# Experts of a two-block decoder layer: neighbouring rows per partition, g2 applied on GpSimd, scattered products added from PSUM

## The chip, the cores and the metric

The kernel runs on one core of a Trainium2 chip. The metric is the device time of one execution in microseconds. The engines are named as in the profile: PE (TensorE, with PEld for its weight loads), DVE (VectorE), ACT (ScalarE), POOL (GpSimd) and SP (SyncE, which issues the loads).

## The reference

Two blocks run one after the other over 256 tokens of 2048 values. The change lies in the last part, a mixture of 16 experts, of which each token uses two:

```python
def moe_ffn(h, router_w, router_bias, w_gate, w_up, w_down):
    ...
    combine = jnp.sum((esel[..., None] == jnp.arange(N_EXPERTS)) * w[..., None], axis=1)
    y = jnp.zeros_like(t)
    for e in range(N_EXPERTS):
        he = jax.nn.silu(t @ w_gate[e]) * (t @ w_up[e])
        y = y + combine[:, e:e + 1] * (he @ w_down[e])
    return y.reshape(b, s, d)
...
h = rmsnorm_2(x, norm2_g[l]) * (1.0 + sc2[:, None]) + sh2[:, None]
x = x + g2[:, None] * moe_ffn(h, router_w, ...)
return rmsnorm_2(x, final_g)
```

`w_gate` and `w_up` are 2048 x 512 for each expert, `w_down` is 512 x 2048, all in 32-bit floats: 4 MB each. `g2` is one row of 2048 values.

## The kernel before

Weights arrive as loads of 1 MB (128 partitions x 2048 values), issued by SP in order into a ring of buffers (`_load`, L128). A load is worked on in two chunks of 1024 columns. For five chunks of six `_split` makes a rounded copy on ACT (L146) and the rest, weight minus copy, on DVE (L147), and PE multiplies with both (L1914, L1915); every sixth chunk goes to PE whole (L1912). `run` hands out the order: it splits up to AHEAD = 4 chunks ahead, does one chunk's products, and then calls `step`, which takes one entry from each background queue. The order on every engine is the order in which the program emits its instructions; nothing is reordered later.

Between the mixers and the experts, `evac_out` adds the mixers' result to x (L1461), squares it (L1466) and multiplies x with its gain row on POOL to give h2 (L1467), in blocks of 512 columns for the two token tiles tt. `after_mix` then scales h2 and adds the row sh2, the first 1024 columns on DVE (L1784), the others on ACT and POOL (L1800, L1801), and picks the experts with some thirty small DVE instructions (L1795 to L1833) that PE waits for (L1836).

The experts go by pairs. `gather` multiplies h2, by blocks of 128 columns, with a selection matrix, so that the tokens of two experts stand as columns (L1898, L1904, L1905); it runs beside the first eight chunks of `down` of every even expert. In the order of emission stand gate and up of expert e (16 chunks) and then `down` of expert e - 1 (8 chunks). `give` adds the two halves of a down result (ACT L2055, DVE L2056) into the tile `out`, 64 rows for each expert of the pair. After `down` of every odd expert a pipeline of eight `scatter` items starts on the queue "out", for two token tiles and four blocks of 512 columns: PE multiplies the combine weights with `out` into a PSUM bank (L2119), DVE multiplies the bank with g2 (L2125), POOL adds that to x (L2129). An item moves on by one stage at each turn; a turn is every second chunk (pad = 1) for all pairs but the last scattered one, where it is every chunk. The pair of experts 14 and 15 is added by other code (`last`), which stays.

PSUM has eight banks; `bank` hands out the one that was given back first. Seven pairs are scattered in this way: 56 items.

Of the kernel before, what the change touches and what calls it, by code (L numbers as in the profile page):

```python
# [13 lines left out]
OP = mybir.AluOpType  # L14
# [3 lines left out]
D = 2048  # L18
# [27 lines left out]
class Kernel:  # L46
# [50 lines left out]
    def add(self, g):  # L97
        a = 0
        while a < len(g.kts):

            kk = min(g.kk if self.loads[1:] else 1, len(g.kts) - a)
            k0 = g.kts[a]
            src = g.w[k0 * 128:(k0 + kk) * 128, g.c0:g.c1].rearrange("(j p) c -> p j c", p=128)
            self.add_load(src, kk * g.C)
            for j in range(kk):
                self.add_chunk(j * g.C, g.C, lambda wh, wl, j=a + j: self._mm(g, j, wh, wl))
            self.count += 1
            if self.every and self.count % self.every == 0 and self.side:
                src, n, use = self.side.popleft()
                self.add_load(src, n)  # L110
                self.chunks.append([len(self.loads) - 1, 0, n, None, use, None])
            a += kk
# [1177 lines left out]
    def mixers(self):  # L1290
        nc, i = self.nc, self.i
        w = i["w_in_2"][0]
# [158 lines left out]
        def evac_out(c0, w):  # L1451
            def evac(b, ps):
                tt, n = divmod(b * 512, w)
                if c0 + b == 0:
                    self.h2 = [self.U(), self.U()]
                s = slice(c0 + n, c0 + n + 512)
                o, m = self.x[tt][:, s], M[c0 // 1024]
                n = s.start % 1024
                t = self.small([128, 512], "ev")
                nc.vector.tensor_mul(t, ps, m[:, n:n + 512])  # L1460
                (nc.vector if tt or c0 else nc.gpsimd).tensor_add(o, o, t)  # L1461
                k = tt * 4 + s.start // 512

                def rest():
                    j = self.small([128, 512], "pts", 4)
                    nc.scalar.activation(j, o, AF.Square, accum_out=self.s2[:, k:k + 1])  # L1466
                    nc.gpsimd.tensor_mul(self.h2[tt][:, s], o, m[:, 1024 + n:1536 + n])  # L1467
                if c0 == 1536:
                    rest()
                else:  # L1470
                    self.bg("out", rest)
                if tt == 1 and s.stop == c0 + w:
                    for kt in range(c0 // 128, s.stop // 128, 2):
                        self.bg("out", lambda kt=kt: self.logits(kt))
                    if c0 == 0:
                        self.bg("out", lambda: (self.free(M[0]), sh2()))
            return evac

        def sh2():
            self.sh2 = self.row(self.mod[3:4, :])  # L1480
# [290 lines left out]
    def after_mix(self):  # L1771

        nc, i = self.nc, self.i
# [5 lines left out]
        nc.vector.tensor_reduce(ss, self.s2[:, 0:8].rearrange("p (t k) -> p t k", t=2), axis=AX.X, op=OP.add)  # L1779
        r = self.rstd(ss, D, 2)  # L1780
        self.table(AF.Sigmoid)
        for tt in range(2):
            h = self.h2[tt][:, 0:1024]
            nc.vector.scalar_tensor_tensor(h, h, r[:, tt:tt + 1], self.sh2[:, 0:1024], op0=OP.mult, op1=OP.add)  # L1784
        t = self.small([128, 256], "ln")
        nc.scalar.copy(t[0:16, :], self.lg[0:16, 0:256])
        self.done(self.lg)
# [5 lines left out]
        for tt in range(2):  # L1793
            e = slice(tt * 16, tt * 16 + 16)
# [3 lines left out]
        for tt in range(2):  # L1798
            h = self.h2[tt][:, 1024:D]
            nc.scalar.activation(h, h, AF.Copy, scale=r[:, tt:tt + 1])  # L1800
            nc.gpsimd.tensor_add(h, h, self.sh2[:, 1024:D])  # L1801
        self.free(self.sh2)
        v3 = lambda t, n: t.rearrange("p (t e) -> p t e", e=n)
        bc = lambda t, n: t.unsqueeze(2).to_broadcast([128, t.shape[1], n])
# [9 lines left out]
        eq, m = sm(32, "req"), sm(2, "rm")  # L1814
# [102 lines left out]
    def experts(self):  # L1917
        nc, i = self.nc, self.i
        E = {}

        def after(q, n, f):
            for _ in range(n):
                self.bg(q, lambda: None)
            self.bg(q, f)

        def gate_up(e):
            st = E[e] = {}

            def mm(key, j, wh, wl):
                if j == 0:  # L1930
                    st[key] = self.bank()
                    if key == "g" and e % 2 == 0:
                        wt = weights(e)
                        after("gu", 3, lambda: turned(e, wt))
                for n in range(2):
                    x = self.XG[:, e % 2, j + n, :]
                    self.both(st[key], x, wh, wl, slice(n * 512, n * 512 + 512), j + n == 0, j + n == 15)
                if j == 0 and key == "g" and e % 2 == 1 and e < 15:
                    self.S = self.slots(e // 2 + 1)
                if j == 14:  # L1940
                    after("gu", 0, lambda: take(e, key))
                    after("gu", 4 if e < 15 else 0, lambda: fold(e, key))
                    if key == "u":
                        after("gu", 0, lambda: hidden(e))
                        after("gu", 1 if e < 15 else 0, lambda: parts(e))

            for key, w in (("g", "exp_w_gate_2"), ("u", "exp_w_up_2")):
                src = i[w][0, e].rearrange("(j p) n -> p j n", p=128)
                for j in range(0, 16, 4):
                    self.add_load(src[:, j:j + 4, :], 2048)  # L1950
                    for n in range(2):
                        self.add_chunk(n * 1024, 1024, lambda wh, wl, key=key, j=j + 2 * n: mm(key, j, wh, wl), n == 1 and whole())

        def whole():

            return len(self.loads) % 3 == 0
# [25 lines left out]
        def weights(e):  # L1982

            w = self.small([128, 256], "bias", 3)
            for tt in range(2):
                for n in range(2):
                    k = tt * 16 + e + n
                    nc.gpsimd.tensor_scalar(w[:, tt * 128 + n * 64:tt * 128 + n * 64 + 64], self.iota,
                                            self.pos_[:, k:k + 1], self.comb[:, k:k + 1],
                                            op0=OP.is_equal, op1=OP.mult)  # L1990
            return w
# [32 lines left out]
        def down(e):  # L2024
            src = i["exp_w_down_2"][0, e].rearrange("(j p) n -> p j n", p=128)
# [33 lines left out]
            def rows(j, c, wh, wl):  # L2059
                if j == 0 and c == 0:  # L2060
                    begin()
                for n in range(2):
                    mm(j, c * 2 + n, wh, wl, slice(n * 512, n * 512 + 512))
                if j == 3 and c == 1 and e % 2 == 1:
                    after("out", 3, lambda: None)
                    self.pipeline("out", [scatter(e - 1, tt, b) for tt in range(2) for b in range(4)], 1, e < 13)

            def columns(b, c, wh, wl):
                if b == 0 and c == 0:
# [36 lines left out]
            for n in range(4):  # L2106
                self.add_load(src[:, n:n + 1, :] if e < 15 else src[:, :, n * 512:n * 512 + 512], 2048)
                for c in range(2):
                    self.add_chunk(c * 1024, 1024,
                                   lambda wh, wl, n=n, c=c: (rows if e < 15 else columns)(n, c, wh, wl), c == 1 and whole())  # L2110

        def scatter(e, tt, b):
            s = slice(b * 512, b * 512 + 512)
            x = self.x[tt][:, s]
            st = {}

            def mm():
                ps = st["ps"] = self.bank()
                nc.tensor.matmul(ps, E[e]["ct"][:, tt * 128:tt * 128 + 128], E[e]["out"][:, s], start=True, stop=True)  # L2119
                if tt == 1 and b == 3:  # L2120
                    self.free(E[e]["out"])

            def mul():
                st["t"] = self.small([128, 512], "ev")
                nc.vector.tensor_mul(st["t"], st["ps"], self.g2[:, s])  # L2125
                self.done(st["ps"])

            def add():
                nc.gpsimd.tensor_add(x, x, st["t"])  # L2129
            return [mm, mul, add]  # L2130

        def new_block():
            self.XG = self.big.tile([128, 2, 16, 128], F32R, name=self.name("xg"), tag="big")
# [25 lines left out]
        for e in range(16):  # L2159
            n = len(self.chunks)  # L2160
# [5 lines left out]
            if e:  # L2166
                n = len(self.chunks)
# [5 lines left out]
    def overflow(self):  # L2173

        nc, i = self.nc, self.i
        for q in ("out", "end0", "end1", "end2", "end3"):
            self.flush(q)
        n = nc.values_load(self.most[0:1, 0:1], min_val=0, max_val=T)
        self.resize(-len(self.ring))
        hT, hid, wts = [self.U(), self.U()], self.U(), deque(self.U() for _ in range(3))  # L2180
        with self.tc.If(n > 64):
# [5 lines left out]
            for kt in range(NKT):  # L2187
                ps = self.bank()
# [10 lines left out]
                return wt  # L2199

            with self.tc.For_i(0, 16, 1) as e:
                w = {k: i[f"exp_w_{k}_2"][0][bass.ds(e, 1)].rearrange("a (j p) n -> p (a j) n", p=128)
                     for k in ("gate", "up", "down")}
                eq = self.small([128, 32], "req", 1)
                c = self.small([128, 2], "rm", 1)
                for tt in range(2):
# [16 lines left out]
                for b in range(2):  # L2223
                    t = self.small([128, 512], "ev")
                    o = hid[:, b * 512:b * 512 + 512]
# [4 lines left out]
                for tt in range(2):  # L2230
# [6 lines left out]
                    for b in range(4):  # L2237
                        t = self.small([128, 512], "ev")
                        s = slice(b * 512, b * 512 + 512)
                        nc.vector.tensor_mul(t, y[b], self.g2[:, s])  # L2240
                        x = self.x[tt][:, s]
                        nc.vector.scalar_tensor_tensor(x, t, c[:, tt:tt + 1], x, op0=OP.mult, op1=OP.add)
                        self.done(y[b])
            for tt in range(2):
                for b in range(4):
                    t = self.small([128, 512], "ev")
# [104 lines left out]
```

## Time and profile before

| what | value |
|---|---|
| median of three runs | 2854.59 us (2854.22 to 2856.4) |
| the profiled execution | 2856.04 us, of which the span 2854.3 us |
| PE, DVE, ACT, POOL busy in the span | 97%, 74%, 50%, 11% |
| granted TensorE clock, mean | 0.987 of 2.4 GHz |
| HBM read | 680.66 MB, 239 GB/s over the span |
| the experts, about | 2240 us to the end |
| loads of gate, up and down | 64 each, 1 MB each |

A row of groups gives line, engine, operation, what is written from what, the count, the busy time and the mean duration of one; then the idle time of the engine before them and who ended it. A row of waits gives who waited for whom, the total in us, the number of waits and the longest. A row of a window gives from and to, the length, the busy time and the count of instructions of each engine, the granted clock, the share of the 16 DMA engines and their rate.

### The profile page before, as it was taken

The page shows a single profiled execution, that of the slowest core. Times are in us where ns is not written, and L with a number is a line of the kernel's source. Part 1 is how long each engine was busy: PE and PEld are TensorE (multiplying, and loading weights), DVE is VectorE, ACT ScalarE, POOL GpSimd, SP SyncE. Part 2 cuts the span into 40 slices and gives each one's busy share as a digit, 9 for nine tenths or more (in the row PEclk, how much of TensorE's full clock was granted, in tenths as well). Part 3 has the DMA queues.
Part 4 walks back from the last instruction along what each step waited for, and adds up shares of the span by engine and source line. Part 5 has one row for each costly group of instructions (what it writes and reads, how often), then busy time and mean ns, then how long its engine had stood idle before and what let it go on. Part 6 is the DMA issues. An engine that isn't in the chain of part 4 may idle for free. (4 is left out here: it accounts for less than half of the span.)

```text
span 2854.3 us, 43859 instructions
## 1 busy us (share of the span) xinstructions
PE 2756.7 (97%) x17766; PEld 2410.4 (84%) x17766; DVE 2106.4 (74%) x2679; ACT 1418.5 (50%) x2100; POOL 315.8 (11%) x286
## 2 busy tenths in 40 slices
PE   8999999999999999999999998999999799999997
PEld 8898999999998999897989797988886676666664
DVE  5566558899767768877777786656555689998998
ACT  5433444334444545434444445345554476666665
POOL 0000100000100000001000102111001202222223
PEclk9999999999999999999999999999999899999999
DMA  7576555566667765676667573745555599989895
GB/s 256 193 275 247 199 215 166 176 235 214 248 233 266 259 228 221 239 263 216 257 216 267 195 253 128 265 128 195 179 202 173 209 372 337 342 324 343 322 342 211
DMA packets 201427, 685.77 MB, mean 240 GB/s; under 512 B 12148, under 2 KB 15332, under 8 KB 180356
## 3 DMA queue, kind: packets, MB, share of 16 engines
q1 hardware_dynamic: 194336, 662.94, 64.3%
q0 software_dynamic: 5680, 19.53, 2.5%
q8 instruction: 141, 2.31, 0.3%
q10 hardware_dynamic: 1203, 0.45, 0.1%
q14 instruction: 67, 0.54, 0.1%
HBM read 680.66 MB, written 2.20 MB: 239 GB/s over the span
## 5 line engine op out<-in xcount | busy, mean ns | idle before, releaser
L147 DVE TENSOR_TENSOR u<-u,u 128x1024 fp32r<-128x1024 f32 (+3 forms) x1064 | 1258.1, 1216 | 393.9 <-ACT u L146 392.2
L146 ACT CAST u<-u 128x1024 fp32r<-128x1024 f32 (+3 forms) x1064 | 1015.3, 995 | 615.6 <-DMA u<-in_w_in_dram 157.3
L181 PE MATMUL ps<-u,u 128*128 128x256 f32 (+1 forms) x2184 | 626.3, 287 | 2.6 <-ACT u L146 1.7
L183 PE MATMUL ps<-u,u 128*128 128x256 f32 (+1 forms) x2184 | 621.1, 284 | 2.5 <-DVE u L147 2.5
L182 PE MATMUL ps<-u,u 128*128 128x256 f32 (+1 forms) x2184 | 621.0, 284 | 0.5
L181 PE MATMUL ps<-big,u 128*128 128x256 f32 (+1 forms) x1672 | 481.4, 288 | 1.2 <-ACT big L1285 0.7
L183 PE MATMUL ps<-big,u 128*128 128x256 f32 (+1 forms) x1672 | 476.6, 285 | 4.3 <-DVE u L147 4.3
L182 PE MATMUL ps<-big,u 128*128 128x256 f32 (+1 forms) x1672 | 476.5, 285 | 0.1
L181 PEld LDWEIGHTS ps<-u,u 128*128 128x128 f32 (+1 forms) x2184 | 420.9, 193 | 11.9 <-issue 6.4
L183 PEld LDWEIGHTS ps<-u,u 128*128 128x128 f32 (+1 forms) x2184 | 420.7, 193 | 4.4 <-DVE u L147 4.3
L182 PEld LDWEIGHTS ps<-u,u 128*128 128x128 f32 (+1 forms) x2184 | 420.9, 193 | 1.7 <-DVE u L1286 1.3
L181 PEld LDWEIGHTS ps<-big,u 128*128 128x128 f32 (+1 forms) x1672 | 322.9, 193 | 13.5 <-issue 7.0
L183 PEld LDWEIGHTS ps<-big,u 128*128 128x128 f32 (+1 forms) x1672 | 322.9, 193 | 5.8 <-DVE u L147 5.6
L182 PEld LDWEIGHTS ps<-big,u 128*128 128x128 f32 (+1 forms) x1672 | 323.0, 193 | 1.1 <-DVE big L1286 0.6
L171 PE MATMUL ps<-u,u 128*128 128x512 f32 x736 | 291.6, 396 | 5.4 <-ACT u L146 5.3
L172 PE MATMUL ps<-u,u 128*128 128x512 f32 x736 | 288.8, 392 | 7.9 <-DVE u L147 7.5
L173 PE MATMUL ps<-u,u 128*128 128x512 f32 x736 | 287.6, 391 | 0.0
L1148 DVE SCALAR_TENSOR_TENSOR u<-u,cols,u 128x2048 f32<-128x2048 f32 x96 | 226.3, 2357 | 5.6 <-DMA u<-in_ada_w_dram 5.5
L1914 PE MATMUL ps<-u,xg 128*128 128x512 f32 x416 | 187.9, 452 | 0.4 <-DVE xg L1905 0.3
L172 PEld LDWEIGHTS ps<-u,u 128*128 128x128 f32 x736 | 138.7, 188 | 39.4 <-DVE u L147 12.4
L171 PEld LDWEIGHTS ps<-u,u 128*128 128x128 f32 x736 | 138.5, 188 | 39.5 <-ACT u L146 8.7
L1915 PE MATMUL ps<-u,xg 128*128 128x512 f32 x416 | 167.7, 403 | 0.8 <-DVE u L147 0.7
(374 smaller groups left out, 3111.5 us busy)
## 6 DMA issues: line engine op xcount, KB each, us to landing
u<-in_w_in_dram SPq DMA_DIRECT2D x128, 1024.0 KB, 5.0
u<-in_ada_w_dram SPq DMA_DIRECT2D x96, 1024.0 KB, 5.4
u<-in_w_up_dram SPq DMA_DIRECT2D x88, 1024.0 KB, 5.4
u<-in_exp_w_gate_dram SPq DMA_DIRECT2D x64, 1024.0 KB, 9.5
u<-in_exp_w_up_dram SPq DMA_DIRECT2D x64, 1024.0 KB, 6.8
u<-in_exp_w_down_dram SPq DMA_DIRECT2D x64, 1024.0 KB, 8.1
u<-in_w_down_dram SPq DMA_DIRECT2D x44, 1024.0 KB, 6.7
u<-in_w_o_dram SPq DMA_DIRECT2D x16, 1024.0 KB, 6.8
```

Source lines behind the costliest of these rows:

```text
L146: self.nc.scalar.copy(wh[:, :width], wt)
L147: self.nc.vector.tensor_sub(wl[:, :width], wt, wh[:, :width].bitcast(F32))
L171: nc.tensor.matmul(o, xh[:, ts], wh[:, cs], start=first, stop=False)
L172: nc.tensor.matmul(o, xh[:, ts], wl[:, cs], start=False, stop=False)
L173: nc.tensor.matmul(o, xl[:, ts], wh[:, cs], start=False, stop=last)
L181: nc.tensor.matmul(o, wh[:, cs], xh, start=first and m % 2 == 0, stop=False, **kw)
L182: nc.tensor.matmul(o, wh[:, cs], xl, start=False, stop=False, **kw)
L183: nc.tensor.matmul(o, wl[:, cs], xh, start=False, stop=last, **kw)
L1148: nc.vector.scalar_tensor_tensor(a, wt, self.col["c"][:, kt:kt + 1], a, op0=OP.mult, op1=OP.add)
L1914: self.nc.tensor.matmul(ps, x, wh[:, s], start=start, stop=False)
L1915: self.nc.tensor.matmul(ps, x, wl[:, s], start=False, stop=stop)
```

## The change

A partition of a gate or up load now takes the rows 16 p + j for neighbouring j, so that the four rows of one load lie side by side in memory (8 KB), in place of rows 128 j + p (four pieces of 2 KB). The columns of h2 are stored in the matching order by the three places that write it, so that block j of 128 columns in h2 holds the values 16 p + j of the model dimension. In the scatter, g2 is multiplied into the rows of `out` before the product, on POOL and once for both token tiles; an empty stage follows; DVE adds the product from PSUM to x. The items go by column block first, then token tile. The fallback for more than 64 tokens per expert, which doesn't run with these inputs, follows the new order of rows.

```diff
                 def rest():
                     ...
-                    nc.gpsimd.tensor_mul(self.h2[tt][:, s], o, m[:, 1024 + n:1536 + n])
+                    h = self.h2[tt].rearrange("t (j p) -> t j p", j=16)[:, :, s.start // 16:s.start // 16 + 32]
+                    nc.gpsimd.tensor_mul(h, o.rearrange("t (p j) -> t j p", j=16),
+                                         m[:, 1024 + n:1536 + n].rearrange("t (p j) -> t j p", j=16))
...
+        sh2 = self.sh2.rearrange("t (p j) -> t j p", j=16)
         for tt in range(2):
-            h = self.h2[tt][:, 0:1024]
-            nc.vector.scalar_tensor_tensor(h, h, r[:, tt:tt + 1], self.sh2[:, 0:1024], op0=OP.mult, op1=OP.add)
+            h = self.h2[tt][:, 0:1024].rearrange("t (j p) -> t j p", j=8)
+            nc.vector.scalar_tensor_tensor(h, h, r[:, tt:tt + 1], sh2[:, 0:8, :], op0=OP.mult, op1=OP.add)
...
             h = self.h2[tt][:, 1024:D]
             nc.scalar.activation(h, h, AF.Copy, scale=r[:, tt:tt + 1])
-            nc.gpsimd.tensor_add(h, h, self.sh2[:, 1024:D])
+            h = h.rearrange("t (j p) -> t j p", j=8)
+            nc.gpsimd.tensor_add(h, h, sh2[:, 8:16, :])
...
             for key, w in (("g", "exp_w_gate_2"), ("u", "exp_w_up_2")):
-                src = i[w][0, e].rearrange("(j p) n -> p j n", p=128)
+                src = i[w][0, e].rearrange("(p j) n -> p j n", j=16)
...
-                    self.pipeline("out", [scatter(e - 1, tt, b) for tt in range(2) for b in range(4)], 1, e < 13)
+                    self.pipeline("out", [scatter(e - 1, tt, b) for b in range(4) for tt in range(2)], 1, e < 13)
...
+            def scale():
+                o = E[e]["out"][:, s]
+                if tt == 0:
+                    nc.gpsimd.tensor_mul(o, o, self.g2[:, s])
+
             def mm():
                 ...
-            def mul():
-                st["t"] = self.small([128, 512], "ev")
-                nc.vector.tensor_mul(st["t"], st["ps"], self.g2[:, s])
+            def add():
+                nc.vector.tensor_add(x, x, st["ps"])
                 self.done(st["ps"])
-
-            def add():
-                nc.gpsimd.tensor_add(x, x, st["t"])
-            return [mm, mul, add]
+            return [scale, lambda: None, mm, add]
```

## Rows read from the trace of the kernel before

**Rows 1.** The page's part 1: busy time of each engine over the span.

```profile
PE 2756.7 (97%) x17766; PEld 2410.4 (84%) x17766; DVE 2106.4 (74%) x2679; ACT 1418.5 (50%) x2100; POOL 315.8 (11%) x286
```

**Rows 2.** Windows: PE, PEld, DVE, ACT, POOL, clock, DMA; the experts, their steady part.

```profile
2240.00:2854.00 614.00, 579.81 (x2504) 406.74 (x2502) 539.01 (x589) 407.36 (x545) 146.59 (x90) 0.98 0.85 317
2320.00:2800.00 480.00, 464.65 (x1982) 324.47 (x1981) 439.62 (x466) 330.44 (x425) 127.03 (x77) 0.99 0.92 342
```

**Rows 3.** Waits from 2320 to 2800 us: us in total, times, longest.

```profile
DVE u L147 <- ACT u L146: 20.0, 28, 3.3
DVE u L2056 <- ACT u L2055: 17.7, 12, 2.9
PEld ps L1915 <- DVE u L147: 16.3, 46, 0.6
...
PE ps L1914 <- DVE ev L2125: 11.4, 6, 2.0
...
ACT u L146 <- DMA u<-in_exp_w_down_dram: 0.5, 1, 0.5
```

**Rows 4.** Line L147, ns min/median/max: the steady part, then 2384 to 2404 us.

```profile
L147 DVE TENSOR_TENSOR u<-u,u x263: 1206/1216/2311, 2319.3 to 2799.2; 128x1024 fp32r<-128x1024 f32 x132
...
L147 DVE TENSOR_TENSOR u<-u,u x15: 1206/1209/1226, 2383.8 to 2402.5; 128x1024 fp32r<-128x1024 f32 x15
```

**Rows 5.** Groups of DVE instructions from 2320 to 2800 us.

```profile
L147 DVE TENSOR_TENSOR u<-u,u 128x1024 fp32r<-128x1024 f32 x263 | 348.9, 1367 | 20.7 <-ACT u L146 20.0
...
L2125 DVE TENSOR_TENSOR ev<-ps,u 128x512 f32<-128x512 f32 x52 | 35.3, 678 | 0.0
```

**Rows 6.** Timeline of DVE and of POOL: start, us, instruction.

```profile
2725.25 3.43 DVE L147 TENSOR_TENSOR u<-u,u 128x1024 fp32r<-128x1024 f32 x2
...
2725.41 2.19 POOL L2129 TENSOR_TENSOR u<-u,ev 128x512 f32<-128x512 f32 x1 [1.76 <-DVE ev L2125]
...
2793.19 16.81 POOL L2129 TENSOR_TENSOR u<-u,ev 128x512 f32<-128x512 f32 x8 [41.33 <-DVE ev L2125]
```

**Rows 7.** Groups of POOL instructions from 2240 us to the end.

```profile
L2129 POOL TENSOR_TENSOR u<-u,ev 128x512 f32<-128x512 f32 x56 | 116.4, 2092 | 418.5 <-DVE ev L2125 418.5
L1988 POOL TENSOR_SCALAR bias<-cst,pos,comb 128x64 f32<-128x64 f32 x29 | 24.6, 864 | 10.5 <-PE ps L1996 10.5
```

**Rows 8.** Line L1071, another DVE add with PSUM, earlier in the kernel.

```profile
L1071 DVE TENSOR_TENSOR u<-u,ps x48: 677/681/689, 1181.6 to 1743.0; 128x512 f32<-128x512 f32 x48
```

**Rows 9.** Group of the scatter's products on PE from 2240 us to the end.

```profile
L2119 PE MATMUL ps<-u,o 128*128 128x512 f32 x112 | 59.2, 610 | 1.7 <-DVE xg L1905 1.7
```

**Rows 10.** Windows with a full queue: gate and up loads land, then down loads.

```profile
2411.00:2421.00 10.00, 10.00 (x37) 6.50 (x36) 9.16 (x14) 9.63 (x13) 0.00 (x0) 1.00 1.06 391
2421.50:2431.00 9.50, 9.50 (x35) 5.88 (x34) 9.50 (x9) 5.94 (x8) 4.37 (x2) 1.00 1.01 417
```

**Rows 11.** Timeline from 2215 to 2234 us: DVE, POOL and PE before the experts.

```profile
2217.77 1.26 DVE L1461 TENSOR_TENSOR u<-u,ev 128x512 f32<-128x512 f32 x1
...
2221.69 2.48 DVE L1784 SCALAR_TENSOR_TENSOR u<-u,rstd,u 128x1024 f32<-128x1024 f32 x2
...
2226.07 4.65 POOL L1801 TENSOR_TENSOR u<-u,u 128x1024 f32<-128x1024 f32 x2 [5.68 <-ACT u L1800]
2226.24 2.21 DVE L1821 TENSOR_TENSOR req<-req,cst 128x8 f32<-128x8 f32 x1
...
2228.68 2.07 DVE L1824 TENSOR_TENSOR rgm<-req,rm 128x8 f32<-128x8 f32 x1
...
2233.80 0.58 PE L1836 MATMUL ps<-sel,cst 128*128 128x16 f32 x2 [9.52 <-DVE sel L1833]
```

**Rows 12.** Two DVE lines on one tile of 256 values: L1182 steps by 16.

```profile
L1182 DVE TENSOR_REDUCE rstd<-ln x1: 580/580/580, 2029.0 to 2029.0; 128x16 f32<-128x256 f32 x1
...
L1179 DVE TENSOR_TENSOR ln<-rw,cols x1: 419/419/419, 2028.2 to 2028.2; 128x256 f32<-128x256 f32 x1
```

More of the change, by code (lines that the diff above doesn't have):

```diff
@@ L2201, in overflow @@
             with self.tc.For_i(0, 16, 1) as e:
-                w = {k: i[f"exp_w_{k}_2"][0][bass.ds(e, 1)].rearrange("a (j p) n -> p (a j) n", p=128)
-                     for k in ("gate", "up", "down")}
+                w = {k: i[f"exp_w_{k}_2"][0][bass.ds(e, 1)].rearrange(rows, p=128)
+                     for k, rows in (("gate", "a (p j) n -> p (a j) n"), ("up", "a (p j) n -> p (a j) n"),
+                                     ("down", "a (j p) n -> p (a j) n"))}
                 eq = self.small([128, 32], "req", 1)
```

## The prediction

> **What bounds the kernel now.** I read first the page's busy shares [rows 1]: PE 97%, DVE 74%. Only the last fifth of the span is touched, so the stages come next [rows 2]: from 2320 to 2800 us, the experts' steady part, PE is busy 464.65 of 480 us and DVE 439.62, that is 91.6%, far above its mean, while DMA stands at 0.92 and 342 GB/s. All three are near their limits, so the list of waits has to say which ends last [rows 3]. Arithmetic waited for a load once, for 0.5 us: the loads run ahead and are not the bound. PE waited for DVE: 11.4 us at the first product of a down projection (six times 2 us, for a PSUM bank that L2125 hands back late), 16.3 us of weight loads for the low parts of L147. That is 27.7 us of waits on DVE in 480. DVE in turn waited 20.0 us for ACT's copies (L146) and 17.7 us for ACT's half of `give`, which both happen where PE is full with gathers. So the stage changes hands: DVE leads in plain gate/up chunks and while the scatter runs, PE in the gathers.
>
> Part of DVE's load is not its own. In a stretch without POOL work 15 L147 take 1206 to 1226 ns, median 1209; over the steady part the longest takes 2311 and their mean is 1367 [rows 4, 5]. The timeline shows why [rows 6]: POOL's add starts at 2725.41 beside an L147, both have two SBUF inputs, the add takes 2.19 us, and two L147 take 3.43 us in place of 2.3. So the price of a POOL add on DVE is (1.367 - 1.209) us x 263 / 52 adds = 0.80 us, and 2.31 - 1.21 = 1.10 us where it hits a full queue of L147.
>
> **Part 1: products added from PSUM by DVE, g2 by POOL.** Removed: 56 adds L2129 on POOL [rows 7] and as many L2125 on DVE. Added: 56 adds of x and PSUM on DVE, of the form of L1071, 681 ns against 678 [rows 5, 8]: 56 x 0.003 = 0.2 us, nothing. Added on POOL: 28 multiplies of the same shape as the adds (only for tt = 0), since 28 products share each scaled row block. So POOL has half the two-input instructions. Price on DVE before: 56 x 0.80 = 44.8 us. After: 28 x 0.80 = 22.4 us if they fall as the adds did, 28 x 1.10 = 30.8 us if all four of a pair run one behind the other as soon as `give` has filled the rows, as the last eight adds do, 16.81 us for 8 without a gap [rows 6]. POOL's queue holds nothing else then, so I take the dear end: DVE saves 44.8 - 30.8 = 14.0 us (22.4 at the other end). Of that, what falls where PE leads is worth nothing. DVE is busy 91.6% of the steady part, and its idle time is where PE leads; the multiplies now move ahead of the gathers, into plain chunks where DVE leads. I take 0.8: 11 us; the ends are 0 and 22.
>
> The wait that is added: the product L2119 needs POOL's multiply. Behind it on PE stand the next chunk's products. The multiply is issued two pipeline steps earlier, four chunks with the pad, one after each chunk of gate or up; the experts' 384 chunks fill some 614 us [rows 2], 1.6 us each, so there are 6.4 us of cover for a multiply of about 2.1 us [rows 7]: free. If that cover is gone (POOL held up), each of 28 costs up to 2 us, 56 us; nothing on POOL's queue does that, its other work there being L1988 at 0.86 us [rows 7], in other chunks.
>
> The pipeline grows by one stage, and a product leaves four chunks later than before. Before, one product of a pair fell into the eight gather chunks; now three do. A product is two instructions, 59.2 us for 56 [rows 9], 1.06 us each. PE does no more work in all; it does two products per pair less where DVE leads and two more where PE leads. I count it at nothing, since the gather stretch loses waits at the same time (the 2 us ones are behind an L147 held by POOL), and price it under the rivals.
>
> **Part 2: neighbouring rows.** A partition of a gate or up load now reads 8 KB in one piece in place of four pieces of 2 KB; `down` has had 8 KB pieces all along. Where the queue is full, 2 KB pieces run at 391 GB/s and 8 KB pieces at 417 GB/s [rows 10]: 1.0486 MB take 2.68 and 2.51 us. There are 128 such loads, 21 us of DMA time. Work waited for loads for 0.5 us [rows 3], so I take 0 to 0.5 us, 0. The Trainium skill, "DMA: Bandwidth & Descriptors", Specifications, calls 512 B and more enough for line rate; by it the loads gain nothing at all, where the rows show 6%.
>
> h2 must be permuted to match, which makes some reads step by 16 elements: both inputs of L1467, and sh2 in L1784 and L1801. These lie between the mixers and the experts, on the path [rows 11]: at the last block POOL's L1467 holds L1461 (1.26 us in place of 0.69), and x's transposes wait for L1461; L1784 ends at 2224.17, just before the routing's first step; the two L1801 hold the routing's L1821 and L1824 for 2.21 and 2.07 us, and PE waits 9.52 us for the routing's end. So a slower read there is paid in full. Price: no row has a stepped POOL read. Lower bound 0. Upper bound from DVE: L1182 reads 256 elements at a step of 16 in 580 ns, L1179 the same tile in order in 419 [rows 12], a factor of 1.38: one L1467 +0.5, two L1784 +1.0, two L1801 2 x 2.33 x 0.38 = +1.8, together 3.3 us. A stepped read has no reason to be free, and POOL is the slower reader; I take 3 us. The six earlier L1467 stand beside a full PE and cost nothing, or 0.5 us each if L1461 is held by them.
>
> The Trainium skill, "GPSIMD Engine Reference", section Performance pitfalls for Q7 kernels, speaks against this part: reads stepping over 8 bytes cost about half as much again. As an estimate by that rule one L1467 and two L1801 would give +0.6 and +2.3 us, some 3 us, close to the bound above. No run here shows it yet.
>
> **Sum.** -11 + 3 + 0 = -8 us, against the profiled execution's own 2856.04 us (span 2854.3, 1.7 us around it): 2848. That execution lies 1.45 us over the median of the runs, 2854.59, so on the median 2846.6.
>
> **Rivals.**
> Same: PE leads more than I think, and the products that moved cost what they are: two per pair in the gather stretch, 2 x 1.06 us x 6 padded pairs = 12.7 us, which eats the 8. Time 2859 with all of it, 2853 with half. For it: PE is busy 97% there [rows 2]. Against it: PE's 27.7 us of waits on DVE [rows 3].
>
> Slower: PSUM banks. In a gather chunk four banks hold the down sums, two the gather, one the folded gate and up, one the product: all eight. Each gather or product then needs the bank that DVE handed back a moment ago, and a DVE that is behind holds PE. The row is the 2 us wait of L1914 for L2125, once per pair, six times [rows 3]. With three products among the gathers in place of one there may be two more such waits in each of six pairs, 2 x 2.0 x 6 = 24 us: 2846.6 + 24 = 2871. It decides if DVE's add comes later than PE's next gather, that is if DVE trails by about a chunk (1.6 us). Against it: without POOL's adds in that stretch DVE trails less.
>
> Faster: the loads bind after all, unseen because waits for several semaphores are booked to the last. Then the 21 us come on top: 2825. Against it: one wait of 0.5 us [rows 3].
>
> The change doesn't do what it says: the loads keep their 2 KB pieces. Since I count nothing for them the forecast stands; the page's packet count would show it.
>
> **How the numbers follow.** Forecast -8, own range 2837 to 2852 (from 0.8 of 22.4 us with free steps to 0.4 of 14 us with steps of 3.3): chance 0.50. Same 0.25, slower 0.15, faster 0.10. Bound for telling from no change 0.2%, 5.7 us: 2848.9 to 2860.3. Faster: 0.38 of the forecast's 0.50, the 0.10 of the loads, 0.02 of others: 0.50. Within: 0.12 of the forecast, 0.18 of the same case: 0.30. Slower: the 0.15 and the rest of the same case: 0.20. The range of 8 in 10 goes from 2828, near the loads' case, to 2866, part of the way into the banks' case.
>
> **What would show it.** L147's mean in the steady part falls from 1367 to 1280 or 1310 ns (right) or stays (wrong); 28 POOL multiplies in groups of four of about 2.2 us; packets of the experts' loads down to about a quarter for gate and up, and DMA near 417 GB/s when full. L1801 above 2.34 us each and L1821, L1824 longer by as much show the step price. PE waits on L2125's successor (the add to x) at L1898 or L2119 in gather chunks would show the banks' case; unchanged DVE idle and no change in time the first rival. A step price far over 1.38, or loads slower by the wider distance between partitions, would make the forecast wrong.

## The result, and the profile after

The changed kernel takes 2888.49 us (median of four, 2885.36 to 2890.15) against 2854.56 us for the kernel before on the same chip: a ratio of 1.0115, 95% interval 1.0099 to 1.0131. It is 34 us slower; 8 us faster was forecast. Its profiled execution took 2890.15 us, with a span of 2888.3 us. Lines of the experts lie five further down in the new file: L1915 is now L1920, L1905 is L1910, L2056 is L2061; the product L2119 is L2130, the multiply on GpSimd L2126, the add from PSUM L2135.

Busy time (part 1 of the page, answering to [rows 1]), and the packets of part 2, which were 201427 before:

```profile
PE 2768.4 (96%) x17766; PEld 2414.8 (84%) x17766; DVE 2094.4 (73%) x2679; ACT 1419.3 (49%) x2100; POOL 290.8 (10%) x258
...
DMA packets 152273, 685.76 MB, mean 237 GB/s; under 512 B 12147, under 2 KB 15331, under 8 KB 114819
```

DVE and POOL have less to do than before, as intended, the loads come in fewer and larger packets (some 49150 fewer; three of four packets of 128 loads on 128 partitions are 49152), and the kernel is slower. The windows of the experts (columns as in [rows 2]) say who lost:

```profile
2240.00:2888.00 648.00, 591.15 (x2530) 412.48 (x2530) 527.44 (x614) 409.58 (x549) 120.66 (x67) 0.97 0.77 302
2320.00:2800.00 480.00, 446.82 (x1881) 307.48 (x1880) 397.95 (x445) 312.77 (x408) 97.35 (x49) 0.98 0.80 317
```

In the steady part every engine is less busy than in [rows 2]: PE 446.82 us of 480 in place of 464.65, DVE 397.95 in place of 439.62. So it isn't more work; engines wait more for each other, and the granted TensorE clock is a little lower (0.98 in place of 0.99; more on that below). The waits from 2320 to 2800 us, answering to [rows 3]:

```profile
ACT u L146 <- PE ps L1920: 72.4, 60, 2.6
DVE u L147 <- ACT u L146: 65.2, 43, 5.0
PEld ps L1920 <- DVE u L147: 48.4, 66, 2.4
...
PE ps L1920 <- DVE u L147: 22.9, 27, 1.9
...
DVE u L2061 <- ACT u L2060: 14.7, 11, 3.7
...
PE ps L2130 <- DVE xg L1910: 10.0, 10, 1.0
```

PE's waits for the low parts of L147 went from 16.3 us to 48.4, as its weight loads show them (the 22.9 us at the products are largely the same waits, seen once more). The six 2 us waits for a PSUM bank in [rows 3] are gone; ten of 1 us at the scatter's product took their place. DVE stands idle for ACT's copies (65.2 us in place of 20.0), and those for PE: the three engines take turns waiting. The groups that answer to [rows 5] and [rows 7]:

```profile
L147 DVE TENSOR_TENSOR u<-u,u 128x1024 fp32r<-128x1024 f32 x247 | 302.1, 1266 | 65.8 <-ACT u L146 65.2
...
L2126 POOL TENSOR_TENSOR u<-u,u 128x512 f32<-128x512 f32 x24 | 48.9, 2049 | 387.0 <-DVE u L2061 387.0
L1993 POOL TENSOR_SCALAR bias<-cst,pos,comb 128x64 f32<-128x64 f32 x24 | 47.9, 2009 | 0.0
```

L147's mean fell from 1367 to 1266 ns, more than the prediction asked of itself, and it didn't help. The timelines of POOL, DVE and PE behind one `down` of an odd expert show why; the last line is that of the slots in the kernel before, over the steady part:

```profile
2430.53 2.32 POOL L2126 TENSOR_TENSOR u<-u,u 128x512 f32<-128x512 f32 x1 [2.21 <-DVE u L2061]
2434.00 4.56 POOL L2126 TENSOR_TENSOR u<-u,u 128x512 f32<-128x512 f32 x2 [1.15 <-DVE u L2061]
...
2431.62 1.58 DVE L1890 TENSOR_TENSOR o<-pos,cst 128x128 f32<-128x128 f32 x2
2433.24 0.68 DVE L2061 TENSOR_TENSOR u<-ps,u 64x512 f32<-64x512 f32 x1
2433.95 1.23 DVE L147 TENSOR_TENSOR u<-u,u 128x1024 fp32r<-128x1024 f32 x1
2435.21 0.69 DVE L2061 TENSOR_TENSOR u<-ps,u 64x512 f32<-64x512 f32 x1
2435.92 9.43 DVE L147 TENSOR_TENSOR u<-u,u 128x1024 fp32r<-128x1024 f32 x7
...
2435.23 0.50 PE L1920 MATMUL ps<-u,xg 128*128 128x512 f32 x1 [1.94 <-DVE u L147]
...
2437.47 0.50 PE L1920 MATMUL ps<-u,xg 128*128 128x512 f32 x1 [1.04 <-DVE u L147]
...
2440.50 1.02 PE L2130 MATMUL ps<-u,o 128*128 128x512 f32 x2
...
L1885 DVE TENSOR_TENSOR o<-pos,cst x12: 284/284/285, 2342.2 to 2714.3; 128x128 f32<-128x128 f32 x12
```

Here DVE has everything at once: the low parts, the four sums of `give` (L2061), the next pair's slots (L1890). Each multiply starts as soon as `give` has filled its rows, so POOL reads SBUF just there; the two slots take 1.58 us together in place of twice 0.284, and PE waits 1.94 and 1.04 us. The first product (L2130) leaves only at 2440.50: PE has nothing else to do in these waits.

To see where the time grows I compared when PE starts the transposes of each pair's weights (L1996 before, L2001 after), once per pair; each kernel's profiled execution minus that of before, in us:

| kernel | 2nd pair (2314.6 before) | 8th pair (2759.8 before) | growth per pair |
|---|---|---|---|
| changed kernel | 9.5 | 34.3 | 4.1 |
| rows alone | 7.6 | 7.4 | 0.0 |
| scatter alone | 2.0 | 29.2 | 4.5 |
| changed, g2 on DVE | 6.6 | 9.2 | 0.4 |
| changed, no multiplies | 5.7 | 8.4 | 0.5 |
| the same, no stages | 6.3 | -9.9 | -2.7 |
| g2 on GpSimd, paced | 9.5 | 16.1 | 1.1 |
| g2 on DVE, at once | 6.0 | 31.1 | 4.2 |
| old rows, g2 on DVE, early | -1.7 | 0.2 | 0.3 |
| old rows, g2 on DVE, spread | 0.0 | -9.5 | -1.6 |

The last columns hold what the experiments below explain: some 8 us ahead of the experts, and some 4 us for each of six pairs.

### The profile page after: what moved, and what is told of

It reads as the page before. It is cut to its first block, busy times and chain, and to the rows that moved or that the text cites. A ratio compares the mean times of both kernels' runs of the same rounds, so it can differ in the third digit from the quotient of the medians.

```text
span 2888.3 us, 43823 instructions
## 1 busy us (share of the span) xinstructions
PE 2768.4 (96%) x17766; PEld 2414.8 (84%) x17766; DVE 2094.4 (73%) x2679; ACT 1419.3 (49%) x2100; POOL 290.8 (10%) x258
## 5 line engine op out<-in xcount | busy, mean ns | idle before, releaser
L147 DVE TENSOR_TENSOR u<-u,u 128x1024 fp32r<-128x1024 f32 (+3 forms) x1064 | 1232.8, 1193 | 445.1 <-ACT u L146 443.3
L172 PE MATMUL ps<-u,u 128*128 128x512 f32 x736 | 291.7, 396 | 10.4 <-DVE u L147 10.4
L171 PE MATMUL ps<-u,u 128*128 128x512 f32 x736 | 294.6, 400 | 5.5 <-ACT u L146 5.3
L173 PE MATMUL ps<-u,u 128*128 128x512 f32 x736 | 291.1, 396 | 0.0
L1920 PE MATMUL ps<-u,xg 128*128 128x512 f32 x416 | 173.7, 418 | 24.6 <-DVE u L147 24.3
L1919 PE MATMUL ps<-u,xg 128*128 128x512 f32 x416 | 189.9, 456 | 0.4 <-DVE xg L1910 0.3
```

The source lines that it names most:

```text
L147: self.nc.vector.tensor_sub(wl[:, :width], wt, wh[:, :width].bitcast(F32))
L171: nc.tensor.matmul(o, xh[:, ts], wh[:, cs], start=first, stop=False)
L172: nc.tensor.matmul(o, xh[:, ts], wl[:, cs], start=False, stop=False)
L173: nc.tensor.matmul(o, xl[:, ts], wh[:, cs], start=False, stop=last)
L1919: self.nc.tensor.matmul(ps, x, wh[:, s], start=start, stop=False)
L1920: self.nc.tensor.matmul(ps, x, wl[:, s], start=False, stop=stop)
```

## The experiments

Times are medians. The twelve kernels ran in three groups of four, each on another chip and beside the kernel before, which had 2855.94, 2856.83 and 2856.03 us there; so a difference between groups is good to about 2 us. The edits are cut to the lines that decide and stand against the changed kernel, unless another is named.

**Which part.** First the rows and h2 without the new scatter, then the new scatter without the rows.

```diff
-            return [scale, lambda: None, mm, add]
+            return [mm, mul, add]
```

> The change came out some 34 us slower than the kernel before. Theory A: the lines in common of the two traces part by about 9 us at the mixers' last blocks and the routing (stepped reads of h2) and then by about 4.5 us for each pair of experts (the new scatter). Rival B: the growth per pair comes from the loads of neighbouring rows. This kernel takes the neighbouring rows and the permuted h2 and keeps the old scatter. A expects +8 to +11 us over the kernel before (2863 to 2866) and nothing lost per pair; B expects +30 us or more (2885 to 2890).

2864.3 us, ratio 1.003 (1.0018 to 1.0042): +8.4 us, and nothing per pair. A holds.

```diff
-                src = i[w][0, e].rearrange("(p j) n -> p j n", j=16)
+                src = i[w][0, e].rearrange("(j p) n -> p j n", p=128)
```

> Only the new scatter (g2 on GpSimd into the rows of two experts, the empty stage, the new order, the add from PSUM on DVE); rows and h2 as before. Theory A expects +23 to +27 us over the kernel before (2878 to 2882), with the loss in the 16 chunks behind each down of an odd expert; B expects -8 to -14 us (2841 to 2847), as the prediction's first part had it.

2884.61 us, ratio 1.0102 (1.0086 to 1.0117): +28.7 us, somewhat over A's range. B falls twice. Taken together the two parts make 37 us, the change 34; the 3 us between are little more than the spread.

**What of the scatter.** The multiplies on DVE, then left out.

```diff
-                    nc.gpsimd.tensor_mul(o, o, self.g2[:, s])
+                    nc.vector.tensor_mul(o, o, self.g2[:, s])
```

> The changed kernel with its 28 multiplies by g2 on DVE in place of GpSimd, all else kept. Theory A1: the loss per pair is GpSimd's multiplies, which all start as soon as give has filled the rows and slow the DVE work there. It expects 15 to 28 us less than the changed kernel (2861 to 2873): the DVE pays some 28 x 0.65 = 18 us of its own for them, part of it hidden. Rival C: the loss is the products and the sums' rows held longer, in the gathers; it expects no gain, 2885 or more.

2867.35 us, ratio 1.004 (1.0026 to 1.0053): 21 us less than the changed kernel.

```diff
-                    nc.gpsimd.tensor_mul(o, o, self.g2[:, s])
+                    pass
```

> The changed kernel with the 28 multiplies by g2 left out altogether (the output lacks that factor), all else kept: it prices the multiplies alone. Theory A1 expects about 28 us less than the changed kernel or more (2850 to 2862), what is left over the kernel before being the stepped reads. Rival C expects at most 5 us less (2883 or more).

2864.05 us, ratio 1.0028 (1.0018 to 1.0038): the multiplies on GpSimd cost 24.4 us, 0.87 each, on DVE 3.3 us. C expected at most 5 us and falls as the price of the multiplies; its products among the gathers come back in the next run. A1's range, 2850 to 2862, is missed by 2 us, too: what is left is level with the rows alone (2864.3): without any multiply the new scatter gains nothing over the old one, though 56 GpSimd adds are gone. That called for the next run.

**The stages.**

```diff
-            return [scale, lambda: None, mm, add]
+            return [mm, add]
```

> The changed kernel without the multiplies by g2 (the output lacks that factor) and without the two stages ahead of the product, so that a product leaves as early as in the kernel before. Without multiplies but with the stages the time was 2864.05 us, no better than the old scatter with the new rows, 2864.3. Theory D: the stages take two products of a pair out of chunks in which PE waits for DVE anyway and put them beside the gathers, where PE is full; giving them back saves 2 x 1.06 us x 6 pairs = 12.7 us, so 2849 to 2855. Rival E: taking the adds off GpSimd is simply worth nothing, since PE doesn't wait for what it frees: 2861 or more.

2843.15 us, ratio 0.9955 (0.9941 to 0.9968): 20.9 us less, more than D had. The waits from 2320 to 2800 us, first with the stages, then without:

```profile
PEld ps L1920 <- DVE u L147: 30.1, 51, 1.2
...
PE ps L1920 <- DVE u L147: 11.5, 18, 0.8
PE ps L2130 <- DVE xg L1910: 10.0, 10, 1.0
```

```profile
PEld ps L1920 <- DVE u L147: 17.6, 50, 0.6
...
PE ps L2130 <- DVE xg L1910: 5.0, 5, 1.0
```

A product needs nothing of DVE's low parts. Where DVE is behind, it fills PE's time, and DVE catches up meanwhile; two stages later it stands among the gathers, where PE is full, and where it waits for a bank that L1910 hands back. The products are paid for where they went, since where they were a wait takes their place: L147's waits are 12.5 us longer with the stages (30.1 against 17.6), as much as D's price of 12.7 us for the products. D didn't have the waits for the bank, 5.0 us more. The two make 17.5 of the 20.9 us; the rest is open.

**The parts put together.** The multiplies on DVE, the products as early as before, the rows as before.

```diff
-                    after("out", 3, lambda: None)
+                    after("out", 1, lambda: None)
...
-            return [scale, lambda: None, mm, add]
+            return [scale, mm, add]
```

> Rows and h2 as before; the new scatter with the multiplies on DVE, without the empty stage, and started two turns' steps earlier, so that each product leaves where it left in the kernel before. Theory D with the priced parts: 2864 (no multiplies, with stages) - 12.7 (stages) - 8.4 (rows as before) + 3.3 (multiplies on DVE) = 2846 us, 2842 to 2850, so some 9 us under the kernel before. Rival E: 2856 or more, since only the rows' 8 us come off the 2867 of the changed kernel with its multiplies on DVE, and DVE's work is now closer together.

2860.07 us, ratio 1.0012 (1.0003 to 1.0021): D misses by 14 us, and the time lies in E's range. The sum had priced the multiply and not the wait for it. With two chunks between multiply and product PE waits for the multiply (L2121 here), behind the low parts on DVE:

```profile
PEld ps L2125 <- DVE u L2121: 20.5, 6, 4.2
...
PE ps L2125 <- DVE u L2121: 17.4, 7, 3.8
```

The two rows show the same waits, at the weight load and at the product: once for each of six pairs, some 3 us, 17 to 20 us in all. (The 38 us in the next expectation add the two rows, which counts them twice.) So the multiplies went onto a queue of their own, three chunks ahead of a pair's first product and four ahead of the others (against the kernel before):

```diff
+                    for b, n in enumerate((0, 2, 3, 3) if e < 13 else (0, 1, 1, 1)):
+                        after("g2", n, lambda b=b: scaled(e - 1, b))
...
+        def scaled(e, b):
+            o = E[e]["out"][:, b * 512:b * 512 + 512]
+            nc.vector.tensor_mul(o, o, self.g2[:, b * 512:b * 512 + 512])
```

> Rows as before, products where they were before, added from PSUM by DVE, and the multiplies by g2 on DVE, issued three chunks ahead of the first product of a pair and four ahead of the others (two in the run that came out at 2860 us, in which PE waited 38 us for them). Theory D: with that lead PE doesn't wait for them; 2843.15 (no multiplies, products early, new rows) - 8.4 (rows as before) + 3.3 to 10 (multiplies on DVE) = 2838 to 2845 us, faster than the kernel before by 12 to 19. Rival I: DVE has no room for 28 x 0.68 us there, whatever the lead: 2852 to 2860.

2844.62 us, ratio 0.996 (0.9946 to 0.9973): faster than the kernel before by 11 us and than the changed one by 44. It is in D's range. PE's waits for the multiplies are gone, and what is left of waits on DVE is near [rows 3], without its 11.4 us for banks:

```profile
PEld ps L1915 <- DVE u L147: 23.1, 47, 1.0
...
PE ps L1915 <- DVE u L147: 5.2, 11, 0.6
PE ps L2125 <- DVE xg L1905: 5.0, 5, 1.0
```

**Engine or place.** GpSimd's multiplies cost 24 us and DVE's 3. But they also stood at different places: DVE runs them where the program emits them, one in four chunks, while GpSimd, with an empty queue, ran them as soon as `give` was done. The next two runs swap this.

```diff
+        self.tick = self.ctile([128, 1], "tick")
...
+                    n = self.pos
+                    while self.chunks[n][5] is None:
+                        n += 1
+                    nc.gpsimd.tensor_copy(self.tick, self.chunks[n][5][:, 0:1].bitcast(F32))
                     nc.gpsimd.tensor_mul(o, o, self.g2[:, s])
```

> The changed kernel, each multiply on GpSimd held back until the low part of the next split chunk is there (a copy of one column of it ahead of the multiply on the same engine), so that the four of a pair start some four chunks apart, as DVE's did in the run with g2 on DVE, and not all at once behind give. Theory J (place): the same 28 multiplies cost 24 us because they run one behind the other where DVE has the sums of give, the slots and the low parts to do; spread out they cost 10 us at most, 2867 to 2875. Rival K (engine): a GpSimd multiply costs DVE its 0.8 to 1.1 us wherever it falls, and that is paid in full: 2882 to 2892.

2869.32 us, ratio 1.0042 (1.0028 to 1.0056): the same 28 multiplies on the same engine now cost 5.3 us, the copies included. J holds. POOL's timeline shows them apart (the copy is the wait); the changed kernel's four run from 2427.03 to 2438.56 us:

```profile
2435.15 1.04 POOL L2130 COPY tick<-u 128x1 f32<-128x1 f32 x1 [5.46 <-DVE u L148]
2436.15 2.27 POOL L2131 TENSOR_TENSOR u<-u,u 128x512 f32<-128x512 f32 x1
2439.63 1.05 POOL L2130 COPY tick<-u 128x1 f32<-128x1 f32 x1 [1.21 <-DVE u L148]
2440.64 1.28 POOL L2131 TENSOR_TENSOR u<-u,u 128x512 f32<-128x512 f32 x1
```

```diff
                 self.done(o)
+                if e % 2 == 1 and e < 15:
+                    t, s = E[e - 1]["out"][:, b * 512:b * 512 + 512], slice(b * 512, b * 512 + 512)
+                    nc.vector.tensor_mul(t, t, self.g2[:, s])
...
-                    nc.gpsimd.tensor_mul(o, o, self.g2[:, s])
+                    pass
```

> The changed kernel with the multiplies on DVE, each right behind the sum of give that fills its rows (four within four chunks), in place of one every four chunks, which came out at 2867.35 us. Theory J (place): four times 0.68 us at the point where DVE is the one PE waits for is paid nearly in full, 7 x 2.7 = 19 us over the run without multiplies, 2877 to 2884. Rival K (engine): on DVE they cost little wherever they stand: 2865 to 2870.

2889.17 us, ratio 1.0115 (1.0099 to 1.013): as slow as the change itself, with GpSimd out of it. 25 us over the run without multiplies, more than the 28 x 0.69 = 19 us that they take, and 5 us over J's range. Place, not engine: K falls in both.

**The clock in the price.** Between the transposes of the 2nd and of the 8th pair all these kernels run the same 1845 PE instructions. Windows from the one start to the other, in us of each profiled execution (idle is the length less busy):

| kernel | length | PE busy | PE idle | granted clock |
|---|---|---|---|---|
| before | 445.15 | 429.81 | 15.34 | 0.99 |
| changed kernel | 469.97 | 437.33 | 32.64 | 0.98 |
| changed, no multiplies | 447.83 | 427.14 | 20.69 | 1.00 |
| the same, no stages | 428.92 | 423.83 | 5.09 | 1.00 |
| g2 on GpSimd, paced | 451.71 | 428.84 | 22.87 | 1.00 |
| g2 on DVE, at once | 470.25 | 440.38 | 29.87 | 0.97 |
| old rows, g2 on DVE, spread | 435.57 | 425.25 | 10.32 | 1.00 |

The multiplies of the changed kernel cost 22.1 us here: 12.0 us in which PE is idle, and 10.2 us in which it is busy longer with the same products. With the multiplies on DVE at once the two are 9.2 and 13.2 us, which is how 19 us of DVE work can cost 25. In the changed kernel's trace the granted clock falls from 2.4 to 1.2 GHz in four stretches between 2320 and 2800 us, some 20 us in all; each begins within 2.5 us of the end of a PE wait for L147 of 1.94 or 1.95 us at a product. The first such wait ends at 2356.12:

```profile
2348.00:2356.00 8.00, 5.78 (x21) 3.46 (x19) 7.66 (x8) 7.86 (x11) 4.63 (x3) 1.00 1.02 426
2357.00:2362.00 5.00, 4.33 (x9) 2.40 (x9) 5.00 (x4) 1.04 (x1) 5.00 (x3) 0.50 0.82 242
```

In the first window two products in a row start 0.23 us apart, in the second 0.43. The wait of the same length at 2435.23 has no such stretch behind it. In the kernels without multiplies and with those of DVE spread out the clock stays at 2.4 GHz from 2320 to 2800 us. That the fall follows from the waits is read from this order; no run sets the two apart.

**The rows' 8.4 us.** The loads alone (against the kernel before), sh2 read in order, and the step moved from the reads of the gain multiply to its write.

```diff
-                src = i[w][0, e].rearrange("(j p) n -> p j n", p=128)
+                src = i[w][0, e].rearrange("(p j) n -> p j n", j=16)
```

> The kernel before with the loads of gate and up by neighbouring rows and h2 left as it was (so the products pair the wrong rows: it prices the loads alone). Theory A: the loads run ahead, so nothing changes: within 2 us of the kernel before. Rival F: the wider pieces do save something under the cost of the permuted h2: 3 to 8 us faster, and the 8.4 us of the rows alone would be 11 to 16 of stepped reads. Rival B: pieces at a wider distance cost something: 3 us slower or more.

2856.0 us, ratio 1.0 (0.9991 to 1.0009): nothing, either way.

```diff
-            h = self.h2[tt][:, 0:1024].rearrange("t (j p) -> t j p", j=8)
-            nc.vector.scalar_tensor_tensor(h, h, r[:, tt:tt + 1], sh2[:, 0:8, :], op0=OP.mult, op1=OP.add)
+            h = self.h2[tt][:, 0:1024]
+            nc.vector.scalar_tensor_tensor(h, h, r[:, tt:tt + 1], self.sh2[:, 0:1024], op0=OP.mult, op1=OP.add)
...
-            h = h.rearrange("t (j p) -> t j p", j=8)
-            nc.gpsimd.tensor_add(h, h, sh2[:, 8:16, :])
+            nc.gpsimd.tensor_add(h, h, self.sh2[:, 1024:D])
```

> The new rows with the old scatter, and sh2 read in order where it is added to h2 (so the wrong values of sh2 are added: it prices the stepped reads of sh2 by DVE and GpSimd apart from those of the gain multiplies). The traces have the two DVE reads 1.3 us and the two GpSimd reads 1.0 us longer in sum, just ahead of the routing. Theory A: 2 to 3 us less than the new rows alone, 2861 to 2862.5, the other 6 us being the gain multiplies beside DVE in the mixers' last blocks. Rival G: the reads of sh2, on the path, are the bulk: 2857 to 2859.

2863.39 us, ratio 1.0023 (1.0014 to 1.0032): between A and no difference from the rows alone; G falls. PE's wait for the routing's end is 9.5 us in this trace and 11.0 in that of the rows alone, so these reads cost some 1.5 us there.

```diff
-                    h = self.h2[tt].rearrange("t (j p) -> t j p", j=16)[:, :, s.start // 16:s.start // 16 + 32]
-                    nc.gpsimd.tensor_mul(h, o.rearrange("t (p j) -> t j p", j=16),
-                                         m[:, 1024 + n:1536 + n].rearrange("t (p j) -> t j p", j=16))
+                    h = self.h2[tt].rearrange("t (j p) -> t p j", j=16)[:, s.start // 16:s.start // 16 + 32, :]
+                    nc.gpsimd.tensor_mul(h, o.rearrange("t (p j) -> t p j", j=16),
+                                         m[:, 1024 + n:1536 + n].rearrange("t (p j) -> t p j", j=16))
```

> The new rows with the old scatter, the gain multiplies on GpSimd reading both inputs in order and writing h2 at a step of 16 values, in place of two stepped reads and a write in order. The loads alone cost nothing (2856.0 against 2856.8) and reading sh2 in order gave back 0.9 of the rows' 8.4 us, so some 7 us are left for the gain multiplies. Theory A: they are the stepped reads, which hold VectorE's work beside them; a stepped write costs GpSimd less, so 4 to 7 us come back (2857 to 2860). Rival H: a step costs the same on either side, or it is something else of the new rows: 2863 or more.

2858.2 us, ratio 1.0005 (0.9996 to 1.0014): some 6 of the 8.4 us come back. A holds. Groups and waits from 2140 to 2245 us, first of the rows alone:

```profile
L1469 POOL TENSOR_TENSOR u<-u,u 128x512 f32<-128x512 f32 x8 | 16.7, 2101 | 39.9 <-DVE u L1461 39.9
...
L1461 DVE TENSOR_TENSOR u<-u,ev 128x512 f32<-128x512 f32 x6 | 8.3, 1379 | 0.2
...
PEld ps L172 <- DVE u L147: 5.4, 1, 5.4
PE ps L172 <- DVE u L147: 5.1, 1, 5.1
```

then with the step in the write:

```profile
L1469 POOL TENSOR_TENSOR u<-u,u 128x512 f32<-128x512 f32 x8 | 11.1, 1400 | 40.6 <-DVE u L1461 40.6
...
L1461 DVE TENSOR_TENSOR u<-u,ev 128x512 f32<-128x512 f32 x6 | 6.1, 1012 | 0.2
...
PEld ps L172 <- DVE u L147: 2.6, 1, 2.6
...
PE ps L172 <- DVE u L147: 2.3, 1, 2.3
```

Two stepped reads take 2101 ns in the mean, a stepped write 1400, and the DVE adds and low parts beside them follow. With the stepped reads PE's wait for L147 in the mixers' output stage is twice as long, and L1461, which x's transposes wait for, takes longer. PE's waits show 2.8 us of the 6 at L147 and 1.4 at the transposes (5.9 against 4.5); the rest isn't seen in them.

## Why the prediction was wrong

Its sum, term by term, against the runs (us). The measured column runs from one kernel to the next, so it adds up to the change by construction; what it tells is the size of each term. The granted clock has no term in the prediction; it is in the measured ones.

| term | predicted | measured | from |
|---|---|---|---|
| 56 adds off GpSimd, products as early as before | -44.8 x 0.8 = -36 | -21 | 2843.15 - 2864.3 |
| pipeline longer, products later | 0 | +21 | 2864.05 - 2843.15 |
| 28 multiplies on GpSimd | 30.8 x 0.8 = +25 | +24 | 2888.49 - 2864.05 |
| stepped reads | +3 | +8 | 2864.3 - 2855.94 |
| loads | 0 | 0, within the last | 2856.0 against 2856.83 |
| sum | -8 | +33 | |

**"The pipeline grows by one stage ... I count it at nothing"** is the step that failed most. The prediction saw that two products per pair move into the gathers, and set the waits lost there against it. The runs show that a product among the low parts is a filler: taken out, its time comes back as PE's waits for L147 (30.1 us with the stages, 17.6 without), and in the gathers it adds 5.0 us of waits for a bank. The first rival had the movement and priced it at 12.7 us, without the banks. Counting it would still have left +5.

**"So the price of a POOL add on DVE is ... 0.80 us"**, with 1.10 for the dear end and times 0.8 for what lies on the path, took its prices from the stage as a whole. The multiplies came out at 0.87 us each, close to the predicted 0.88; that is luck in part, since some 10 of the 24 us are products at the lower clock, and it is a price of the place behind `give`. Spread out, the same instruction costs 5.3 / 28 = 0.19 us. The adds of before were spread by their wait for L2125, so they were worth less: 21.2 / 56 = 0.38 us each, the bank waits of [rows 3] that went with them (11.4 us) included. The prediction saw the multiplies move "ahead of the gathers, into plain chunks where DVE leads" and made of it only a share of 0.8; it is the place where they cost most in these runs. With the measured -21 for the adds and +24 for the multiplies part 1 was a loss even with the stages at nothing.

**Wait of the product for POOL, "free"**: right for the change. No wait of L2130 for L2126 stands in the list. That cover is needed is shown, for a multiply on DVE, by the run with two chunks of it, in which PE waited some 3 us once per pair.

**Stepped reads, 3 us**: the part at the routing fits (2.2 us with the gain's step moved to the write, a ratio whose interval takes in 1, against +1.0 and +1.8; L1801 as L1806 takes 2.85 us in place of 2.34, L1784 as L1788 1.94 in place of 1.28). What failed is "the six earlier L1467 stand beside a full PE and cost nothing": PE is full there but draws on L147, which stands beside L1467 on DVE; some 6 us. The way was in the prediction as an aside, "or 0.5 us each if L1461 is held by them", and wasn't counted: the six L1461 on DVE take 1379 ns in the mean in place of 1012. The median L1467 goes from 1287 to 1990 ns (L1469), a factor of 1.55. The Trainium skill, "GPSIMD Engine Reference", Performance pitfalls for Q7 kernels, says half as much again; the trace agrees, where the prediction's bound, DVE's 1.38, was too low. For L1801, with one of two inputs stepped, the factor is 1.22, below both.

**Loads, 0**: right. With a full queue they ran at 424 GB/s after the change (2411 to 2421 us) against 391 [rows 10], and the loads alone changed nothing. By the Trainium skill, "DMA: Bandwidth & Descriptors", Specifications, the pieces would have gained nothing at all; the rate disagrees, the time doesn't.

**Rivals.** The bank waits of the slower rival stayed small: the six of 2 us vanished, ten of 1 us at the products took their place, 10.0 us against 11.4. It ended on the right side with a mechanism that wasn't the cause. No rival had the multiplies' place or the clock.

**What the profile would show**: L147's mean fell as "right" asked. It was the wrong witness: a mean over the stage can't tell a place with slack from one without. The wait list of PE for L147 would have told.

What stays open: the new scatter costs 28.7 us on the old rows and 24.2 on the new ones, little more than the spread between groups of runs; 3 of the 21 us of the stages; and whether the clock falls because of PE's waits, as its order in the trace suggests.

## What to carry to other kernels

Price an instruction by the place where it will run, not by a mean over the stage: the same 28 multiplies cost 24 us behind `give` and 5 us spread out on GpSimd, 25 and 3 on DVE. GpSimd, with an empty queue, ran its work here as soon as the input was there; if that is the tight spot, it needs a wait built in, or an engine whose order holds it back. And work that doesn't depend on the lagging engine is worth something where that engine lags: moved to a stage where everything is full it costs its time, because the wait that it had hidden comes back. Where PE's waits grow, look at the granted clock too: in the changed kernel the same products took some 10 us longer.

## What the runs showed of the hardware

- GpSimd is held off by an unbroken run of DVE instructions with two SBUF inputs, and DVE doesn't notice. In the run that took 2844.62 us the four multiplies that make the weights (L1988, 128 x 64) took 19.55 us, one of them 14.88, while DVE ran twelve L147 without a gap; DVE's L147 in that stretch stayed at 1209 to 1256 ns. First POOL, then DVE, then line L147 there:

```profile
2387.32 19.55 POOL L1988 TENSOR_SCALAR bias<-cst,pos,comb 128x64 f32<-128x64 f32 x4 [52.59 <-PE ps L1996]
...
2388.05 13.70 DVE L147 TENSOR_TENSOR u<-u,u 128x1024 fp32r<-128x1024 f32 x12
...
L147 DVE TENSOR_TENSOR u<-u,u x15: 1209/1210/1256, 2390.3 to 2407.7; 128x1024 fp32r<-128x1024 f32 x15
```

  In the kernel before the median of these is 578 ns. In [rows 6] it is DVE's L147 that gets longer beside a POOL add. That which of the two loses depends on who has its next instruction ready is a guess that no run tests; POOL's spans are rough, but the two lists agree on the order.
- For GpSimd a stepped write of 128 x 512 costs what one in order does (median 1294 against 1287 ns), two stepped reads 1990 ns. Lines of the kernel before, the changed one and the one with the step in the write:

```profile
L1467 POOL TENSOR_TENSOR u<-u,u x8: 1267/1287/1744, 2159.2 to 2219.1; 128x512 f32<-128x512 f32 x8
...
L1469 POOL TENSOR_TENSOR u<-u,u x8: 1883/1990/2575, 2162.6 to 2228.1; 128x512 f32<-128x512 f32 x8
...
L1469 POOL TENSOR_TENSOR u<-u,u x8: 1275/1294/1754, 2157.0 to 2218.3; 128x512 f32<-128x512 f32 x8
```

- DVE's scale-and-add of 128 x 1024 with one input stepped (L1788) takes 1.94 us in place of 1.28.
